# Residual gate prepared beside the spatial stage and kept in DRAM, its memory given to weights and gates, attention's gates two units ahead

## The chip, the cores and the metric

The kernel runs on one core of a Trainium2 chip. Its time is device microseconds of one execution; the time before is the median of three runs, 1124.19 us (1122.96 to 1124.32). The engines are TensorE (PE; its weight loads are shown as PEld), VectorE (DVE), ScalarE (ACT), GpSimd (POOL) and SyncE (SP, which here only issues DMAs; GpSimd issues some as well). Each works off its own queue of instructions in order; they wait for each other on semaphores.

## What is computed

One block of a bidirectional encoder on 1024 tokens of width 1024, all in float32. Cut to what matters:

```
mod = silu(c) @ w_ada + b_ada;  shift, scale, gate = split(mod, 3)
h = rmsnorm(x, norm_g) * (1 + scale) + shift
q, k, v, z_gla, ra_f, ra_b, u, vs, z_gmlp, m_gla, m_gmlp = split(h @ w_in)
log_a = max(log_sigmoid(ra @ alpha_w + alpha_b) / 16, -1.25)       # one per direction
o = gla(q, k, v, log_a_f) + flip(gla(flip(q), flip(k), flip(v), flip(log_a_b), strict))
y_gla = (rmsnorm(o) * gla_norm_g * silu(z_gla)) @ w_br_gla
vs = layernorm(gelu(vs));  sg = per 128 tokens and group: gmlp_ws @ vs + gmlp_bs
y_gmlp = (gelu(u) * sg * silu(z_gmlp)) @ w_br_gmlp
merged = sigmoid(m_gla) * y_gla + sigmoid(m_gmlp) * y_gmlp
out = rmsnorm(x + gate * (merged @ w_out), final_g)
```

gla is gated linear attention in chunks of 64 tokens, 4 heads: b is the running sum of log_a inside a chunk, q * exp(b) and k * exp(-b) give the scores of a chunk, and a state of 128x256 a head is carried on with k * exp(b_last - b) and v.

## The kernel before

Tokens and columns are cut into tiles of 128 and 512. Every product of h or of a branch with a weight is made from high and low halves of both sides (a hi part rounded for TensorE and a lo part for the remainder), hence three matmuls for each: hi x hi, lo x hi, hi x lo. The halves are split by a cast on ScalarE (L175, names ending in h) and a subtraction on VectorE (L176, names ending in l).

The program is written with a tile library. A scheduler simulates it and sets the order of each engine's queue and the slots of each tile; the text is only where it starts from. Tiles live in rings of equal slots: 4 KB a partition for what lasts (h, 30 slots) and for weights (w, 11 slots, `w4`), 2 KB (s, 16 slots, `w2`), 1 KB (q, 12 slots, `w1`). A new tile waits until the last reader of the tile that had its slot is done. The accumulators in PSUM are eight: three `pd`, two `pm`, two `po`, one `pk`.

The stages, by the clock of the profiled execution:

1. Front, 0 to 75 us. Root mean squares of the tokens (`norm_x`, statistics ms at L220), the modulation from w_ada (`ada`), h transposed and split (`make_h`), in three groups of tokens, 0 to 3, 4 and 5, 6 and 7. `spread(g)` (L294) multiplies by a matrix of ones to bring the factors rd of a group's tokens across all partitions. The matmuls of the first half of vs run between.
2. 75 to 180 us: second half of vs (`vs1`), its layer norm, the spatial product (`spatial`, L440 to L450, results sg to DRAM by GpSimd), and v of heads 0 and 1 (`dense_v0`, `dense_v`, L502 to L513; the halves vh, vl lie in the 1 KB ring until SP has stored them).
3. 180 to 600 us: 20 pairs of 128-column blocks of u, z_gmlp, m and z_gla (`pair`). Each is a two by two block product with seven instead of eight multiplications: sums of weights on GpSimd (L574 to L581), sums of h quarters (T1 to T4) made once, and accumulators X (pd), Y (po) and Z (pk). Z is filled by L551 to L553 twice a pair; the last thing read from it is added on VectorE (L607, u), and the next pair's Z starts after that. Between the first pairs stand the residual gate and the small weights of the decay (`low_rank_weights`, kept in ST). The gate multiplies rows of its weights by silu(c) and adds them on VectorE (gacc, L680: eight 512 KB loads wg, one at a time), sums over partitions by a matmul with ones (L689), adds the bias and keeps the row across all partitions in the tile `gate`.
4. 600 to 925 us: attention, 16 units of a head, a direction and half of the tokens. `front_a` makes a unit's gates: decay (L785 on TensorE), three ScalarE activations, a scan on VectorE (L794, L796), then q and k times their exponentials (L810 to L813). `front_b` makes the scores (L822), `front_c` transposes the keys (L832). Four `step`s per unit carry the state (L840 to L842 into pk, L857 and L859 on VectorE) and in the forward direction make the outputs. Between them `dense` takes one piece each of other products from a list of filler jobs: q, k and v of the next heads, and the gMLP branch's output. A unit's gates are made one unit ahead.
5. 925 to 1027 us: the attention branch's output ya (L1156 to L1158), merged with the other branch on VectorE (L1138 to L1141: ta and y2 are read back from DRAM, the merge tile is split into mh and ml). It goes by eight column blocks j and two halves of the tokens.
6. From 1027 us: the output weights (`dense_o`, L211 to L213 with weights th, tl and left side mh, ml). Each of eight 512 KB pieces is loaded (ws), scaled by the gate on GpSimd (L1186) and split. Three tokens begin before the others are ready. x is loaded again (res, L1191, into slots that ya's left side had), added, normalised and stored.

Of the kernel before, what the change touches and what calls it, by code (L numbers as in the profile page):

```python
# [13 lines left out]
ALU = mybir.AluOpType  # L14
# [30 lines left out]
def hybrid_block_kernel(ctx: ExitStack, tc: tile.TileContext, x, wf, wt, wada, wgate, wvr, wst, alpha, abias,  # L45
# [29 lines left out]
    z_d = dram("z_d", [KC, P, T])  # L75
    b12_d = dram("b12_d", [4, P, 1024])
# [35 lines left out]
    ST = cp.tile([P, T], F32R, name="ST")  # L112
    gate = cp.tile([P, D], F32, name="gate")

# [338 lines left out]
    for b in range(2):  # L453
        pw = pm()
        TE.matmul(pw, lhsT=ones, rhs=wsT[:, 4 * b:4 * b + 4, :].rearrange("p g t -> p (g t)"), start=True, stop=True)
        for i in range(4):
            g = 4 * b + i
            V.scalar_tensor_tensor(out=bsb[:, g, :], in0=pw[:, i * P:(i + 1) * P],
                                   scalar=pcol[:, PC_LB + g:PC_LB + g + 1], in1=bsb[:, g, :], op0=ALU.mult,
                                   op1=ALU.add)  # L460
    for t in range(4, 8):
        vs1(t)
    spatial(1)
    for t in range(4):
        vs1(t)
# [41 lines left out]
    def v_steps(acc, pieces, t):  # L507
        for k in range(KC):
            hi, lo = pieces[k]
            TE.matmul(acc, lhsT=H.hi_t(k, t), rhs=hi, start=(k == 0), stop=False)  # L510
            TE.matmul(acc, lhsT=H.hi_t(k, t), rhs=lo, start=False, stop=False)  # L511
            TE.matmul(acc, lhsT=H.lo_t(k, t), rhs=hi, start=False, stop=(k == KC - 1))  # L512
# [152 lines left out]

    def residual_gate():

        gth, gsc = (hp.tile([P, 8], F32, name=n) for n in ("gth", "gsc"))
        V.tensor_scalar(gn, pcol[:, PC_GN:PC_GN + 8], 0.5, None, op0=ALU.mult)
        S.activation(gth, pcol[:, PC_C:PC_C + 8], AF.Tanh, scale=0.5)  # L670
        V.scalar_tensor_tensor(out=gsc, in0=gth, scalar=1.0, in1=pcol[:, PC_C:PC_C + 8], op0=ALU.add, op1=ALU.mult)
        V.tensor_scalar(gsc, gsc, 0.5, None, op0=ALU.mult)
        gacc = ht([P, D], F32, "gacc")
        for k in range(KC):
            wg = ht([P, D], F32, "wg")
            nc.sync.dma_start(wg, wgate[k])
            if k == 0:
                S.activation(gacc, wg, AF.Copy, scale=gsc[:, 0:1])
            else:
                V.scalar_tensor_tensor(out=gacc, in0=wg, scalar=gsc[:, k:k + 1], in1=gacc, op0=ALU.mult, op1=ALU.add)  # L680
        return gacc

    def residual_gate_end(gacc):
        bg = ht([P, D], F32, "bg")
        nc.sync.dma_start(bg, prows[PR_BG].partition_broadcast(P))
        for b in range(2):
            pg = pm()
            sl = slice(b * 512, b * 512 + 512)
            TE.matmul(pg, lhsT=ones, rhs=gacc[:, sl], start=True, stop=True)  # L689
            V.tensor_tensor(out=gate[:, sl], in0=pg, in1=bg[:, sl], op=ALU.add)  # L690

            S.mul(gate[:, sl], gate[:, sl], 0.5)
# [18 lines left out]
    pair_z(2)  # L711
    pair_z(3)
# [317 lines left out]
    def gg_second():  # L1030
# [39 lines left out]
    front_a(0, 0)  # L1070
    dense(3)
    front_b(0, 0)
    dense(1)
    front_c(0, 0)
    for n, (h, u) in enumerate(order):
        q = QUOTA[n]
# [7 lines left out]
        if nxt:  # L1084
            front_a(*nxt)
# [97 lines left out]

    def scale_cols(w, b):
        w3 = w.rearrange("p (k c) -> p k c", k=2)
        G.tensor_tensor(out=w3, in0=w3, in1=gate[:, b * 512:b * 512 + 512].unsqueeze(1).broadcast_to([P, 2, 512]),  # L1186
# [138 lines left out]
```

## Time and profile before

| | |
|---|---|
| time, median of 3 runs | 1124.19 us (1122.96 to 1124.32) |
| profiled execution, own time | 1123.92 us |
| its span | 1121.9 us |
| busy: PE, PEld, DVE, ACT, POOL | 1068.2, 894.4, 641.8, 413.3, 272.7 us |
| moved by DMA | 152.27 MB, 136 GB/s over the span |
| instructions on PE | 5292 matmuls, 5292 weight loads |

The page's busy times are sums over one execution. In rows with an arrow, the left name is the tile that the waiting instruction writes, the right one the instruction that let it go and its line. "Idle before" in square brackets is the time for which the engine had nothing to do ahead of that row. A granted clock of 0.5 means that TensorE ran at half speed.

### The profile page before, as it was taken

Reading aid. Unit: us, or ns where it says so; the run is one execution under the profiler, and the core shown is the slowest. Engines: PE = TensorE matmul, PEld = TensorE weight load, DVE = VectorE, ACT = ScalarE, POOL = GpSimd, SP = SyncE. Lnnn points to the kernel's source line nnn. Section 1 sums busy time; section 2 is a strip of 40 time slices with the busy share of each in tenths; the row PEclk is TensorE's granted clock in tenths of the full one; section 3 lists DMA queues with packets and bytes.
Section 4 is the critical chain, followed back from the end, with each engine's and each line's share of the span. In section 5 each row is a group of like instructions: output and inputs, shape, how many; then the busy total and the mean of one; then the engine's idle time right before and its main releaser. Section 6 shows DMA issues by size and latency. Waiting matters only on the chain.

```text
span 1121.9 us, 14019 instructions
## 1 busy us (share of the span) xinstructions
PE 1068.2 (95%) x5292; PEld 894.4 (80%) x5292; DVE 641.8 (57%) x953; ACT 413.3 (37%) x720; POOL 272.7 (24%) x302
## 2 busy tenths in 40 slices
PE   6889999899999999999999999899989899999997
PEld 4768899678878787877888898798778778888886
DVE  5865568554476555665463466556767664744422
ACT  4453334143332332323233335445536344311222
POOL 2211214443433424343321001001101010012610
PEclk9999999999999999999999999899989899999999
DMA  9541236533233232243336026137525248526112
GB/s 359 186 150 61 85 134 209 192 121 122 75 122 108 100 122 103 92 153 108 118 132 244 1 67 225 39 100 245 191 85 178 86 152 289 189 75 225 38 57 94
DMA packets 55572, 152.27 MB, mean 136 GB/s; under 512 B 7279, under 2 KB 15471, under 8 KB 55506
## 3 DMA queue, kind: packets, MB, share of 16 engines
q1 hardware_dynamic: 40898, 102.42, 26.0%
q0 software_dynamic: 14608, 48.97, 12.2%
q8 instruction: 41, 0.67, 0.2%
q14 instruction: 25, 0.20, 0.1%
HBM read 108.37 MB, written 42.99 MB: 135 GB/s over the span
## 4 chain that ended last, share of the span: by engine, by line
PE 77%; DVE 8%; issue 7%; DMA 3%; ACT 3%; POOL 1%; SPq 0%; POOLq 0%; DVEq 0%; ACTq 0%
PE po L553 4%; PE pd L211 4%; PE pd L212 4%; PE po L551 4%; PE po L552 4%; PE pd L213 4%; PE pd L961 4%; PE pd L962 4%; PE pd L963 4%; PE pk L551 3%; PE pd L553 3%; PE pk L553 3%; PE pd L551 3%; PE pd L552 3%; PE pk L552 3%
## 5 line engine op out<-in xcount | busy, mean ns | idle before, releaser
L511 PE MATMUL pd<-tvl,hh 128*128 128x256 f32 (+1 forms) x256 | 74.6, 292 | 4.0 <-DVE tvl L176 4.0
L510 PE MATMUL pd<-tvh,hh 128*128 128x256 f32 (+1 forms) x256 | 74.7, 292 | 0.8 <-DVE vl L502 0.8
L512 PE MATMUL pd<-tvh,hl 128*128 128x256 f32 (+1 forms) x256 | 74.6, 291 | 0.0
L552 PE MATMUL pd<-hl,ah 128*128 128x512 f32 x160 | 62.3, 390 | 0.0
L553 PE MATMUL pd<-hh,al 128*128 128x512 f32 x160 | 62.2, 389 | 0.0
L551 PE MATMUL pd<-hh,ah 128*128 128x512 f32 x160 | 62.2, 390 | 0.0
L511 PEld LDWEIGHTS pd<-tvl,hh 128*128 128x128 f32 x256 | 49.6, 194 | 4.4 <-DVE tvl L176 4.2
L961 PE MATMUL pd<-ggh,wh 128*128 128x512 f32 x128 | 53.2, 415 | 0.0
L963 PE MATMUL pd<-ggh,wl 128*128 128x512 f32 x128 | 52.1, 408 | 0.0
L962 PE MATMUL pd<-ggl,wh 128*128 128x512 f32 x128 | 51.9, 406 | 0.0
L510 PEld LDWEIGHTS pd<-tvh,hh 128*128 128x128 f32 x256 | 49.6, 194 | 1.3 <-DVE vl L502 1.0
L574 POOL TENSOR_TENSOR wsum<-wb 128x512 f32<-128x512 f32 x20 | 29.5, 1477 | 86.1 <-PE po L552 38.6
L512 PEld LDWEIGHTS pd<-tvh,hl 128*128 128x128 f32 x256 | 49.7, 194 | 0.1
L1158 PE MATMUL pd<-gl,wh 128*128 128x512 f32 x128 | 49.7, 390 | 0.0
L1157 PE MATMUL pd<-gh,wl 128*128 128x512 f32 x128 | 49.7, 389 | 0.0
L1156 PE MATMUL pd<-gh,wh 128*128 128x512 f32 x128 | 49.6, 389 | 0.0
L175 ACT CAST ah<-wa 128x1024 fp32r<-128x1024 f32 x20 | 21.0, 1051 | 73.0 <-PE po L553 52.7
L604 DVE TENSOR_TENSOR p<-po,p 128x512 f32<-128x512 f32 x20 | 13.8, 691 | 58.2 <-PE po L553 58.2
L212 PE MATMUL pd<-tl,mh 128*128 128x512 f32 x120 | 46.8, 391 | 0.0
L221 POOL TENSOR_TENSOR r<-ms,nhalf 128x1 f32<-128x1 f32 (+1 forms) x24 | 20.2, 841 | 109.2 <-DVE ms L220 107.1
L211 PE MATMUL pd<-th,mh 128*128 128x512 f32 x120 | 46.7, 391 | 0.0
L176 DVE TENSOR_TENSOR wl<-ws,wh 128x1024 fp32r<-128x1024 f32 x24 | 29.3, 1221 | 30.2 <-ACT wh L175 16.6
(317 smaller groups left out, 3146.0 us busy)
## 6 DMA issues: line engine op xcount, KB each, us to landing
ws<-in_wf SPq DMA_DIRECT2D x24, 512.0 KB, 4.5
ws<-in_wt SPq DMA_DIRECT2D x22, 512.0 KB, 4.0
wa<-in_wf SPq DMA_DIRECT2D x20, 512.0 KB, 3.6
wb<-in_wf SPq DMA_DIRECT2D x20, 512.0 KB, 4.2
wa<-in_wada SPq DMA_DIRECT2D x16, 512.0 KB, 7.7
xn<-in_x SPq DMA_DIRECT2D x8, 512.0 KB, 8.3
sg_d<-sg POOLq DMA_DIRECT2D x16, 256.0 KB, 2.4
vh_d<-vh SPq DMA_DIRECT2D x32, 128.0 KB, 2.6
```

The costliest lines, as they stand in the source:

```text
L211: TE.matmul(acc, lhsT=xh, rhs=hi[:, k % 2, :], start=(k == 0), stop=False)
L212: TE.matmul(acc, lhsT=xh, rhs=lo[:, k % 2, :], start=False, stop=False)
L510: TE.matmul(acc, lhsT=H.hi_t(k, t), rhs=hi, start=(k == 0), stop=False)
L511: TE.matmul(acc, lhsT=H.hi_t(k, t), rhs=lo, start=False, stop=False)
L512: TE.matmul(acc, lhsT=H.lo_t(k, t), rhs=hi, start=False, stop=(k == KC - 1))
L551: TE.matmul(acc, lhsT=a, rhs=xh(k), start=(first and k == 0), stop=False, skip_group_check=not first)
L552: TE.matmul(acc, lhsT=a, rhs=xl(k), start=False, stop=False, skip_group_check=not first)
L553: TE.matmul(acc, lhsT=b, rhs=xh(k), start=False, stop=(k == 3), skip_group_check=not first)
L961: TE.matmul(acc, lhsT=hi, rhs=x.hi(k, half), start=(k == 0), stop=False)
L962: TE.matmul(acc, lhsT=hi, rhs=x.lo(k, half), start=False, stop=False)
L963: TE.matmul(acc, lhsT=lo, rhs=x.hi(k, half), start=False, stop=(k == KC - 1))
L1157: TE.matmul(acc, lhsT=lo[:, k, :], rhs=GO.hi(k, half), start=False, stop=False)
```

## The change

Seven edits in one:

- The residual gate is worked out between the two halves of the spatial stage, from sixteen loads of 256 KB in 2 KB slots; its matmuls and bias come in the middle of v of head 0, the finished row (2 x 512) is stored to DRAM, and near the end GpSimd loads it again into two 2 KB slots across all partitions.
- The tile `gate` and ST no longer lie in fixed memory: ST takes a weight slot and is made after the third of the last four pairs.
- Rings: weights 11 to 13 slots, 2 KB 16 to 18, 1 KB 12 to 10. v of heads 2 and 3 takes its weights from the weight ring.
- The first pair of u and z comes after the second pair of m.
- Front: the second `spread` comes one step later, the statistics of tokens 6 and 7 come inside the loop.
- Attention: two units' gates are made before the first unit; in the loop those of unit n + 2 come between steps 2 and 3 of unit n.
- The scratch for GpSimd's DMAs is halved.

```diff
-    gate = cp.tile([P, D], F32, name="gate")
-        return hp.tile(shape, dtype, tag="w", bufs=11, name=nm(name))
+        return hp.tile(shape, dtype, tag="w", bufs=13, name=nm(name))
-        return hp.tile(shape, dtype, tag="s", bufs=16, name=nm(name))
+        return hp.tile(shape, dtype, tag="s", bufs=18, name=nm(name))
-        return hp.tile(shape, dtype, tag="q", bufs=12, name=nm(name))
+        return hp.tile(shape, dtype, tag="q", bufs=10, name=nm(name))
...
+        if k == 3:
             spread(1)
-        if k >= 2:
-            make_h(k - 2, 1, abs_[k - 2])
-            steps(k - 2, 1)
-    norm_x(6)
-    norm_x(7)
+        if k == 5:
+            for t in range(6, 8):
+                norm_x(t)
+        for i in {3: (0, 1)}.get(k, (k - 2,) if k > 3 else ()):
+            make_h(i, 1, abs_[i])
+            steps(i, 1)
     spread(2)
...
+    def residual_gate():
...
+        gacc = [w2([P, 512], F32, "gacc") for _ in range(2)]
+        for k in range(KC):
+            for b in range(2):
+                wg = w2([P, 512], F32, "wg")
+                nc.sync.dma_start(wg, wgate[k, :, b * 512:b * 512 + 512])
+                if k == 0:
+                    S.activation(gacc[b], wg, AF.Copy, scale=gsc[:, 0:1])
+                else:
+                    V.scalar_tensor_tensor(out=gacc[b], in0=wg, scalar=gsc[:, k:k + 1], in1=gacc[b], op0=ALU.mult,
+                                           op1=ALU.add)
+        return gacc
+
+    def residual_gate_end(gacc, ins):
+        with tc.issue_after(ins.ins):
+            pg = [pm() for _ in range(2)]
+            for b in range(2):
+                TE.matmul(pg[b], lhsT=ones, rhs=gacc[b], start=True, stop=True)
+        for b in range(2):
+            bg = w2([P, 512], F32, "bg")
+            nc.sync.dma_start(bg, prows[PR_BG, b * 512:b * 512 + 512].partition_broadcast(P))
+            V.tensor_tensor(out=bg, in0=pg[b], in1=bg, op=ALU.add)
+            S.mul(bg, bg, 0.5)
+            nc.sync.dma_start(gate_d[b:b + 1, :], bg[0:1, :])
...
     spatial(1)
+    gacc = residual_gate()
...
+            if t == TOKENS[4]:
+                residual_gate_end(gacc, i)
...
+        ST = w4([P, T], F32R, "ST")
...
     pair_m(FB_MB, tb_d, 0)
-    gacc = residual_gate()
     pair_m(FB_MB, tb_d, 1)
+    pair_uz(0)
     pair_m(FB_MB, tb_d, 2)
     pair_m(FB_MB, tb_d, 3)
-    residual_gate_end(gacc)
-    low_rank_weights()
-    pair_uz(0)
     pair_uz(1)
...
     pair_z(2)
+    ST = low_rank_weights()
     pair_z(3)
...
-            (lambda: v_weights(2, ht), run_v(2)),
+            (lambda: v_weights(2, w4), run_v(2)),
-            (lambda: v_weights(3, ht), run_v(3)),
+            (lambda: v_weights(3, w4), run_v(3)),
...
-    front_a(0, 0)
-    dense(3)
-    front_b(0, 0)
+    front_a(*order[0])
+    dense(2)
+    front_a(*order[1])
     dense(1)
-    front_c(0, 0)
+    front_b(*order[0])
+    dense(1)
+    front_c(*order[0])
...
-        if nxt:
-            front_a(*nxt)
...
         step(h, u, 2)
+        if n + 2 < len(order):
+            front_a(*order[n + 2])
         dense(1)
...
+    gate = [w2([P, 512], F32, "gate") for _ in range(2)]
+    for b in range(2):
+        G.dma_start(gate[b], gate_d[b].partition_broadcast(P))
...
-    nc = _bacc.Bacc("TRN2", target_bir_lowering=False, num_devices=1, dynamic_dma_scratch_size=4096)
+    nc = _bacc.Bacc("TRN2", target_bir_lowering=False, num_devices=1, dynamic_dma_scratch_size=2048)
```

The edits shift lines by up to 35 in the changed text, and the scheduler orders anew. Three places in its order follow; each row is a line, an operation, the tile it writes and those it reads. Numbers behind names only tell tiles of one name apart.

TensorE between two pairs, before: pk_2019 is one pair's Z, pk_2152 the next one's, pd_2226 the next one's X.

```order
1097 L552 MATMUL pk_2019<-hl_108,fh_1956 128x512
1098 L553 MATMUL pk_2019<-hh_107,fl_1957 128x512
1099 L551 MATMUL pd_2226<-hh_93,ah_2209 128x512
1100 L552 MATMUL pd_2226<-hl_94,ah_2209 128x512
1101 L551 MATMUL pk_2152<-t0h_1468,sh_2080 128x512
1102 L552 MATMUL pk_2152<-t0l_1469,sh_2080 128x512
```

And now, from the same pair's last Z product (1099) to the next one's first (1112):

```order
1099 L589 MATMUL pk_2057<-hh_106,fl_1995 128x512
1100 L589 MATMUL pd_2258<-hh_92,al_2242 128x512
1101 L587 MATMUL pd_2258<-hh_92,ah_2241 128x512
1102 L588 MATMUL pd_2258<-hl_93,ah_2241 128x512
1103 L589 MATMUL pd_2258<-hh_92,al_2242 128x512
1104 L587 MATMUL pd_2258<-hh_96,ah_2241 128x512
...
1110 L587 MATMUL po_2273<-t1h_1544,sh_2245 128x512
1111 L588 MATMUL po_2273<-t1l_1545,sh_2245 128x512
1112 L587 MATMUL pk_2190<-t0h_1537,sh_2120 128x512
```

Two matmuls between became twelve: ten more of X and two of Y were drawn ahead. Over all 19 boundaries the number was 2 nine times, 4 once, 8 four times and 22 or 24 five times; now it is 12 or more at each.

VectorE in attention, before, at the second split of v's weights for head 3 (tvl_5618, for matmuls that come right after the state product pk_5702): the rows L801 to L813 are the gates of the next unit, L859 state steps of the running one.

```order
575 L801 COPY c_978_5576<-b_5574 128x8
576 L859 SCALAR_TENSOR_TENSOR s_5706<-s_5687,dec_5403,pk_5702 128x256
577 L807 TENSOR_TENSOR b_5574<-b_5574,c_978_5576 128x4x64
578 L806 TENSOR_TENSOR dec_5580<-e_979_5578 128x4
579 L811 TENSOR_TENSOR qh_5583<-qh_5583,qk_4688 128x512
580 L176 TENSOR_TENSOR tvl_5618<-ws_5615,tvh_5617 128x1024
581 L813 TENSOR_TENSOR b_5574<-b_5574,qk_4769 128x512
```

And now (tvl_5647 is the same split, L867 the state step, L809 to L821 the gates of the same unit):

```order
573 L815 TENSOR_TENSOR b_5570<-b_5570,c_983_5572 128x4x64
574 L867 SCALAR_TENSOR_TENSOR s_5552<-s_5515,dec_5163,pk_5548 128x256
575 L174 TENSOR_TENSOR tvl_5647<-ws_5644,tvh_5646 128x1024
576 L814 TENSOR_TENSOR dec_5576<-e_984_5574 128x4
577 L819 TENSOR_TENSOR qh_5579<-qh_5579,qk_4717 128x512
578 L844 TENSOR_TENSOR kel_5610<-pm_5604,keh_5609 128x512
579 L821 TENSOR_TENSOR b_5570<-b_5570,qk_4798 128x512
...
588 L867 SCALAR_TENSOR_TENSOR s_5687<-s_5654,dec_5374,pk_5683 128x256
```

The gates and the split stand ahead of the running unit's state steps, which come from row 588 on; the state step at row 574 belongs to the unit before it.

The end, SP and ScalarE. Before, SP (in_wt are output weights, res is x, ta the merge's factor of the last column block, second half):

```order
245 L169 DMA ws_8307<-in_wt 128x1024
246 L169 DMA ws_8314<-in_wt 128x1024
247 L169 DMA ws_8321<-in_wt 128x1024
248 L169 DMA ws_8328<-in_wt 128x1024
249 L1191 DMA res_8404<-in_x 128x1024
...
256 L1191 DMA res_8598<-in_x 128x1024
257 L1136 DMA ta_8298<-ta_d 128x512
258 L1137 DMA y_1507_8297<-y_d 128x512
```

And now:

```order
254 L167 DMA ws_8340<-in_wt 128x1024
255 L1145 DMA ta_8292<-ta_d 128x512
256 L1146 DMA y_1513_8291<-y_d 128x512
257 L1204 DMA res_8437<-in_x 128x1024
...
264 L1204 DMA res_8631<-in_x 128x1024
265 L1145 DMA ta_8327<-ta_d 128x512
266 L1146 DMA y_1518_8326<-y_d 128x512
267 L167 DMA ws_8347<-in_wt 128x1024
268 L167 DMA ws_8354<-in_wt 128x1024
269 L167 DMA ws_8361<-in_wt 128x1024
```

ScalarE before (th is a piece of the output weights, mh a merge tile):

```order
604 L175 CAST th_8324<-ws_8321 128x1024
605 L1140 CAST mh_8186<-ta_8189 128x512
606 L1140 CAST mh_8186<-ta_8222 128x512
607 L175 CAST th_8331<-ws_8328 128x1024
608 L1140 CAST mh_8260<-ta_8263 128x512
609 L1140 CAST mh_8295<-ta_8298 128x512
```

And now:

```order
604 L1149 CAST mh_8215<-ta_8218 128x512
605 L1149 CAST mh_8215<-ta_8251 128x512
606 L1149 CAST mh_8289<-ta_8292 128x512
607 L1149 CAST mh_8324<-ta_8327 128x512
608 L173 CAST th_8343<-ws_8340 128x1024
609 L173 CAST th_8350<-ws_8347 128x1024
```

Of the first four pieces of the output weights, three moved behind x and the last ta, and their casts behind the last merge tile. VectorE's four subtractions tl moved likewise. On TensorE three products with th_8343 stand right behind the last product of ya, then the first with tl_8344.

More of the change, by code (lines that the diff above doesn't have):

```diff
@@ L75, in hybrid_block_kernel @@
     z_d = dram("z_d", [KC, P, T])
+    gate_d = dram("gate_d", [2, 512])
     b12_d = dram("b12_d", [4, P, 1024])
@@ L110, in hybrid_block_kernel @@
     pcol = cp.tile([P, NPC], F32, name="pcol")
-    ST = cp.tile([P, T], F32R, name="ST")
-    gate = cp.tile([P, D], F32, name="gate")
     gn = cp.tile([P, 8], F32, name="gn")
@@ L460, in hybrid_block_kernel @@
                                    op1=ALU.add)
+    def residual_gate():
+        gth, gsc = (hp.tile([P, 8], F32, name=n) for n in ("gth", "gsc"))
+        V.tensor_scalar(gn, pcol[:, PC_GN:PC_GN + 8], 0.5, None, op0=ALU.mult)
+        S.activation(gth, pcol[:, PC_C:PC_C + 8], AF.Tanh, scale=0.5)
+        V.scalar_tensor_tensor(out=gsc, in0=gth, scalar=1.0, in1=pcol[:, PC_C:PC_C + 8], op0=ALU.add, op1=ALU.mult)
+        V.tensor_scalar(gsc, gsc, 0.5, None, op0=ALU.mult)
+        gacc = [w2([P, 512], F32, "gacc") for _ in range(2)]
[20 more added lines that the diff above has]
+            nc.sync.dma_start(gate_d[b:b + 1, :], bg[0:1, :])
     for t in range(4, 8):
@@ L511, in v_steps @@
             TE.matmul(acc, lhsT=H.hi_t(k, t), rhs=lo, start=False, stop=False)
-            TE.matmul(acc, lhsT=H.lo_t(k, t), rhs=hi, start=False, stop=(k == KC - 1))
+            i = TE.matmul(acc, lhsT=H.lo_t(k, t), rhs=hi, start=False, stop=(k == KC - 1))
+        return i
     TOKENS = (4, 5, 6, 7, 0, 1, 2, 3)
@@ L518, in dense_v0 @@
             acc = pd()[:, 0:NV0]
-            v_steps(acc, v0_w, t)
+            i = v_steps(acc, v0_w, t)
+            if t == TOKENS[4]:
+                residual_gate_end(gacc, i)
             S.copy(ra[:, t, :], acc[:, HV:NV0])
@@ L664, in low_rank_weights @@
                                in1=sa[96:128, :], op0=ALU.mult, op1=ALU.add)
[L666 to L692, printed above, removed]
+        return ST
     pair_m(FB_MB, tb_d, 0)
-    gacc = residual_gate()
     pair_m(FB_MB, tb_d, 1)
+    pair_uz(0)
     pair_m(FB_MB, tb_d, 2)
     pair_m(FB_MB, tb_d, 3)
-    residual_gate_end(gacc)
-    low_rank_weights()
-    pair_uz(0)
     pair_uz(1)
@@ L1069, in hybrid_block_kernel @@
     dense(4)
-    front_a(0, 0)
-    dense(3)
-    front_b(0, 0)
+    front_a(*order[0])
+    dense(2)
+    front_a(*order[1])
     dense(1)
-    front_c(0, 0)
+    front_b(*order[0])
+    dense(1)
+    front_c(*order[0])
     for n, (h, u) in enumerate(order):
-        q = QUOTA[n]
         nxt = order[n + 1] if n + 1 < len(order) else None
@@ L1094, in hybrid_block_kernel @@
         step(h, u, 1)
-        dense(q - 3)
+        dense(QUOTA[n] - 3)
         if nxt:
@@ L1182, in hybrid_block_kernel @@
     ms = [None] * NT
+    gate = [w2([P, 512], F32, "gate") for _ in range(2)]
+    for b in range(2):
+        G.dma_start(gate[b], gate_d[b].partition_broadcast(P))
     def scale_cols(w, b):
         w3 = w.rearrange("p (k c) -> p k c", k=2)
-        G.tensor_tensor(out=w3, in0=w3, in1=gate[:, b * 512:b * 512 + 512].unsqueeze(1).broadcast_to([P, 2, 512]),
+        G.tensor_tensor(out=w3, in0=w3, in1=gate[b].unsqueeze(1).broadcast_to([P, 2, 512]),
                         op=ALU.mult)
```

## The prediction

> **What bounds the kernel now.** I read the busy totals first, then who made TensorE wait, then the same time by stages.
>
> ```profile
> PE 1068.2 (95%) x5292; PEld 894.4 (80%) x5292; DVE 641.8 (57%) x953; ACT 413.3 (37%) x720; POOL 272.7 (24%) x302
> ```
>
> TensorE is the bound: 95% busy. The change leaves its products as they are, so all that can move is its idle time, 1121.9 - 1068.2 = 53.7 us, and the time in which it runs at half clock. The view of waits, for TensorE alone (total us, times, longest):
>
> ```profile
> PE pm L822 <- DVE b L813: 6.1, 2, 4.0
> PE pk L551 <- DVE u L607: 6.1, 13, 1.0
> PE pd L511 <- DVE tvl L176: 4.0, 1, 4.0
> PE pm L689 <- DVE gacc L680: 3.9, 1, 3.9
> PE pm L294 <- DVE ms L220: 3.3, 1, 3.3
> PE pk L840 <- DVE s L859: 3.0, 6, 0.8
> PE pm L294 <- DVE rd L260: 2.0, 1, 2.0
> ```
>
> Nearly all of it ends on VectorE, at places where TensorE's queue has too little work between a request and its answer. By stages (length, busy us and count of TensorE, weight loads, VectorE, ScalarE, GpSimd, then granted clock, DMA share, GB/s):
>
> ```profile
> core 0: us, PE busy (x) PEld busy (x) DVE busy (x) ACT busy (x) POOL busy (x), PEclk, DMA share, GB/s
> 0.00:75.00 75.00, 57.80 (x252) 43.78 (x253) 50.03 (x110) 34.84 (x59) 18.82 (x22) 1.00 0.58 219
> 75.00:180.00 105.00, 105.00 (x644) 94.52 (x643) 68.61 (x113) 38.10 (x59) 19.53 (x29) 1.00 0.37 130
> 180.00:240.00 60.00, 53.39 (x278) 44.23 (x277) 36.51 (x38) 19.08 (x28) 28.20 (x25) 0.97 0.52 167
> 240.00:600.00 360.00, 353.92 (x1540) 287.44 (x1539) 204.42 (x236) 120.97 (x168) 133.29 (x146) 1.00 0.33 115
> 600.00:700.00 100.00, 99.31 (x581) 87.40 (x581) 50.09 (x91) 43.30 (x87) 6.49 (x11) 1.00 0.38 136
> 700.00:730.00 30.00, 24.54 (x146) 22.15 (x145) 17.15 (x29) 13.25 (x30) 2.73 (x4) 0.89 0.10 36
> 730.00:800.00 70.00, 69.18 (x428) 61.86 (x427) 45.67 (x81) 40.41 (x86) 7.77 (x13) 1.00 0.56 185
> 800.00:830.00 30.00, 24.11 (x111) 19.88 (x110) 17.83 (x30) 9.09 (x19) 3.06 (x6) 0.83 0.30 106
> 865.00:885.00 20.00, 17.54 (x75) 13.94 (x74) 11.81 (x21) 8.06 (x17) 3.26 (x5) 0.83 0.44 144
> 885.00:925.00 40.00, 37.97 (x200) 31.14 (x199) 27.62 (x50) 14.88 (x37) 4.32 (x7) 1.00 0.34 114
> 925.00:1027.00 102.00, 101.96 (x458) 84.37 (x458) 53.58 (x70) 31.09 (x48) 12.35 (x8) 1.00 0.53 185
> ```
>
> Idle (length less busy): front 17.2, the gate's stretch 180 to 240 6.6, the pairs 6.1, attention 0.7 + 5.5 + 0.8 + 5.9 + 2.5 + 2.0 = 17.4, then none up to 1027. The clock falls below 1 just where the long waits are. Cut finer, the stretches behind two of the 4.0 us waits, and the spacing of 256-wide matmuls before and in the first of them:
>
> ```profile
> 721.40:727.50 6.10, 6.10 (x29) 6.10 (x30) 0.93 (x2) 0.94 (x3) 0.00 (x0) 0.51 0.14 47
> 816.80:823.00 6.20, 6.16 (x19) 5.22 (x20) 3.84 (x7) 0.62 (x1) 0.55 (x1) 0.50 0.12 45
> ```
>
> ```profile
> 711.91 0.28 PE L512 MATMUL pd<-tvh,hl 128*128 128x256 f32 x1
> 712.03 0.28 PE L510 MATMUL pd<-tvh,hh 128*128 128x256 f32 x1
> ...
> 722.17 0.41 PE L511 MATMUL pd<-tvl,hh 128*128 128x256 f32 x1
> 722.38 0.41 PE L512 MATMUL pd<-tvh,hl 128*128 128x256 f32 x1
> ```
>
> Full busy, but at 0.21 us a matmul in place of 0.12: of each 0.21 us 0.09 is lost, 43%. So a wait of 4.0 us costs 4.0 + 0.43 x 6.1 = 6.6 us. [...]
>
> **The change, part by part.** The sum is made against the profiled execution's own 1123.92 us (span 1121.9 and 2.0 around it); the median of the runs, 1124.19, is 0.3 above it. A measurement of this kernel can tell about 0.2%, 2.2 us, from no change.
>
> *Front.* The second spread now comes one step later, and the statistics of tokens 6 and 7 two steps earlier. The waits at stake are the 3.3 (ms) and 2.0 us (rd) of L294. The first should go: VectorE gets that work with more than a step of matmuls ahead of it; the second may only shift. Bounds 0 and -5.3; I take -3.0, little short of the one wait that loses its cause. Work saved here does reach the end, since 75 to 180 is 105.00 busy of 105.
>
> *Residual gate.* Its matmul waits 3.9 us at L689, and products held up by the same VectorE queue bring the stretch to 6.6 us idle; clock 0.97 of 60 us is 1.8 us short, that is 3.6 us at half clock, worth 0.43 x 3.6 = 1.5. All that goes: 8.1 us. The cause is a chain of loads, one at a time (view of waits, VectorE):
>
> ```profile
> DVE gacc L680 <- DMA wg<-in_wgate: 17.7, 7, 5.2
> ```
>
> The work returns inside 120 to 180: 14 sums of 128x512 at about 0.69 us (a row of that form stands below) are 9.7 us more on VectorE, whose 68.6 of 105 become 78; and 16 loads, 4 MB, enter SP's queue ahead of nearly all stores of v, at 130 GB/s moved so far. What waits behind them: the stores free ten small slots, enough for five tokens of v, then VectorE stops at the next low half, and TensorE after its three accumulators. That cover is eight tokens of work; if it fails I put the loss at one landing as slow as below (9.9 us) less what is covered. Bounds 0 and +8; I take +1.7, because the loads' slots come free before v begins. Sum -6.4. Writing the row to DRAM and reading it back adds four small transfers with nothing due for hundreds of us: 0.
>
> *Pairs.* The 6.1 us of L551 behind u (L607) are 13 waits of up to 1.0 us: one accumulator, two matmuls of cover (the order shows 2, 4 or 8 at the boundaries that wait). Now at least 12 stand there; the spacing of 512-wide matmuls is 0.23 us (1027.15 to 1027.38, quoted below), so cover grows by 10 x 0.23 = 2.3 us, more than the longest wait. Bounds 0 and -6.1; I take -5.5. The two extra 4 KB slots are what lets the next weights be split that early.
>
> *Attention.* Gates two units ahead: in VectorE's order the weight split tvl that cost 4.0 us now stands ahead of the state steps that it used to follow, and the scores' operands (L813) come a unit earlier. At stake 17.4 us idle and half clock: (0.11 x 30 + 0.17 x 30 + 0.17 x 20) / 0.5 = 23.6 us, of which TensorE idled through 0 to 10 (the three long waits are 10.1); 0.43 x 23.6 = 10.1 down to 0.43 x 13.6 = 5.8, say 7.9. What stays: the last units, where no filler is left (2.0 in 885 to 925), and new short waits, since a unit's last state steps now queue behind the gates of two units on: 3.0 (as much as L859 costs today). One of the three half-clock stretches I leave in. So -(17.4 - 5.0) - 7.9 x 2/3 = -17.7; bounds -25.3 and 0.
>
> *The end: a new wait.* In SP's order three of the four first-half pieces of the output weights moved behind eight loads of x (4 MB); in ScalarE's order all four casts (th), in VectorE's all four remainders (tl) moved behind the last tile of the merge. Before, these casts were interleaved and TensorE went straight over. The rows there:
>
> ```profile
> 1022.75 1.05 ACT L175 CAST th<-ws 128x1024 fp32r<-128x1024 f32 x1 [3.01 <-POOL ws L1186]
> ```
>
> ```profile
> 1027.15 0.39 PE L1158 MATMUL pd<-gl,wh 128*128 128x512 f32 x1
> 1027.38 0.39 PE L211 MATMUL pd<-th,mh 128*128 128x512 f32 x1
> 1027.41 1.22 DVE L176 TENSOR_TENSOR tl<-ws,th 128x1024 fp32r<-128x1024 f32 x1 [2.37 <-PE pd L1157]
> ...
> 1033.10 0.69 DVE L1138 SCALAR_TENSOR_TENSOR ta<-ta,pd 128x512 f32<-128x512 f32 x1 [4.46 <-DMA ta<-ta_d]
> 1033.82 0.69 DVE L1139 TENSOR_TENSOR ta<-ta,y 128x512 f32<-128x512 f32 x1
> 1034.55 0.62 ACT L1140 CAST mh<-ta 128x512 fp32r<-128x512 f32 x1 [10.23 <-DVE ta L1139]
> ...
> 1035.05 2.40 POOL L1186 TENSOR_TENSOR ws<-ws,gate 128x1024 f32<-128x1024 f32 x1 [12.34 <-DMA ws<-in_wt]
> ```
>
> ```profile
> res<-in_x SPq DMA_DIRECT2D x8, 512.0 KB, 7.9
> ...
> ta<-ta_d SPq DMA_DIRECT2D x1, 256.0 KB, 9.9
> ```
>
> The last tile ta is loaded behind the x loads and lands 9.9 us after its issue, so VectorE reaches it at 1033.10 and the cast mh ends at 1035.17. Today that hurts nobody: the first cast stood ahead of it, and three tokens of matmuls ran meanwhile. Now th comes next: 1035.2 + 1.05 = 1036.2, against 1027.38: 8.8 us of idle. Three matmuls need th alone (0.7 us), the fourth tl, 1.22 after th: +0.6. Then half clock, as behind the 4.0 us waits: 0.43 x 6.1 = 2.6. Together +12.0. The next pieces keep up: each feeds 18 matmuls, 4.1 us, and costs GpSimd 2.40. Bounds: +8.8 without the rest, and +16 if the three pieces issued right behind (1.5 MB) delay ta as the 4 MB ahead of it do: 9.9 x 1.5 / 4 = 3.7.
>
> *Smaller edits.* Halved scratch for GpSimd's DMAs, slots moved between sizes: 0. [...]
>
> Sum: 1123.9 - 3.0 - 6.4 - 5.5 - 17.7 + 12.0 = 1103.3.
>
> **The rivals.**
>
> *The end hardly stalls*, because ta lands like the other fifteen. Its loads by landing:
>
> ```profile
> DMA to landing us min/median/max: 2.6/3.8/9.9
> ```
>
> At 3.8 the 8.8 us shrink to 2.7, with 0.6 for tl and no half clock: 1103.3 - 12.0 + 3.3 = 1095; with no stall at all 1091. For it: the first piece itself is loaded ahead of x. Against: the maximum is this very load, behind the same eight.
>
> *Attention's waits only move.* Two units' gates must be held at once, while the ring of small slots shrank from 12 to 10; if they come free too late, VectorE does the gates no earlier than today. Then attention yields perhaps 3 us: 1103.3 + 14.7 = 1118. Against: the waits named above each have their cause moved in the order.
>
> *Slower: the gates get in front of the state.* Place: VectorE between a unit's third and fourth state step. The gates' work there, from first to last row today:
>
> ```profile
> 810.85 0.69 DVE L790 SCALAR_TENSOR_TENSOR e<-pm,e 128x512 f32<-128x512 f32 x1
> ...
> 814.56 0.16 DVE L806 TENSOR_TENSOR dec<-e 128x4 f32<-128x4 f32 x1
> ```
>
> 3.9 us, 0.9 of it state steps: 2.9 us in front of the state that TensorE's next product needs. Exposed in 14 units, that is 41 us in place of the 25.3 lost now: 1103.3 + 17.7 + 41 - 25.3 = 1137. Slower than 1126.1 it is from (25.3 + 1126.1 - 1121.0) / 14 = 2.2 us per unit, when hardly any filler stands between; one filler piece of eight matmuls covers 1.8 of the 2.9, which is why I think it unlikely.
>
> *It does not do what it says:* the gate's loads cost in v what they saved (+6.4) and the front only shifts (+3): 1113, still faster.
>
> **How the numbers follow.** Forecast 0.55 with its own range 1095 to 1113 (bounds of the parts, not all at one end); little or no stall at the end 0.13; attention only moved 0.17; slower by the state 0.08; the gate and front idle 0.07. Range 1088 to 1120, leaving out the slower case, half of what is beyond 1118, and the lowest corner. Faster 0.87; within 0.2% 0.04, from the upper edge of the attention rival; slower 0.09.
>
> **What would show it.** Right: no wait on gacc; the waits behind u gone or under 1 us in all; clock 1.00 from 600 to 900; a gap of 9 to 13 us between the last merge product (L1165 to L1167 now) and the first product of the output weights, with a half-clock stretch behind it. Wrong: waits on the state (s) growing past 10 us, an idle stretch in the v products, or no gap at the end.

## The result

The changed kernel takes 1096.08 us (median of 4 runs, 1094.35 to 1098.20) against 1123.58 us of the kernel before beside it: 0.976 of the time, 95% interval 0.973 to 0.979. It is faster by 2.4%. The forecast was 1103.3 with a range of 1088 to 1120; the gain was forecast as 20.6 us and is 27.5.

The busy totals of the changed kernel:

```profile
PE 1057.6 (97%) x5292; PEld 892.7 (82%) x5292; DVE 641.1 (59%) x960; ACT 412.1 (38%) x721; POOL 276.1 (25%) x304
```

TensorE does the same 5292 matmuls; in a span of 1095.3 us it idles 37.7 us, where it idled 53.7. Of the 26.6 us that the span lost, 16.0 are idle time and 10.6 are busy time. Little of the 10.6 is half clock: the mean granted clock is 0.987 over the span before and 0.988 over this one, short of full clock by 14.6 us and 13.1 us, a difference of 1.5. The rest is mostly starts of matmuls that come late while the row of the matmul ahead still counts as busy; for the pairs this is worked out further below. The view of waits of the changed kernel, TensorE alone (total us, times, longest):

```profile
PE pd L209 <- ACT th L173: 7.8, 1, 7.8
PE pd L241 <- DMA crow<-in_prows: 4.2, 1, 4.2
PE pd L210 <- DVE tl L174: 3.5, 1, 3.5
PE pm L830 <- DVE b L821: 2.6, 1, 2.6
PE pm L306 <- DVE rd L258: 2.0, 2, 1.1
...
PE pd L969 <- ACT wh L173: 1.8, 1, 1.8
...
PE pk L587 <- DVE u L643: 1.1, 1, 1.1
```

The waits on gacc, on tvl and on ms are gone, that on u (13 times before) happens once. What leads the list now is new: th and tl at the start of the output weights. The second row is the first matmul of all, which waits for its input in both kernels. The same by stages (length, busy us and count of TensorE, weight loads, VectorE, ScalarE, GpSimd, then granted clock, DMA share, GB/s):

```profile
0.00:75.00 75.00, 62.48 (x260) 48.37 (x261) 50.26 (x109) 34.69 (x58) 19.49 (x21) 0.95 0.58 223
75.00:180.00 105.00, 105.00 (x648) 94.38 (x647) 78.45 (x129) 41.35 (x63) 22.25 (x32) 1.00 0.49 171
180.00:240.00 60.00, 60.00 (x314) 51.33 (x313) 25.78 (x34) 20.06 (x30) 20.77 (x21) 1.00 0.34 115
240.00:600.00 360.00, 358.86 (x1579) 295.01 (x1578) 203.97 (x241) 125.64 (x172) 140.52 (x155) 1.00 0.37 128
600.00:700.00 100.00, 100.00 (x638) 90.54 (x637) 64.42 (x116) 52.64 (x115) 7.56 (x12) 1.00 0.31 105
700.00:800.00 100.00, 99.42 (x591) 87.30 (x590) 71.36 (x124) 49.98 (x109) 10.28 (x17) 1.00 0.47 158
800.00:925.00 125.00, 119.22 (x600) 100.13 (x599) 77.60 (x123) 53.90 (x114) 13.83 (x21) 0.99 0.54 184
925.00:1020.00 95.00, 83.65 (x353) 68.14 (x352) 43.80 (x47) 15.60 (x25) 20.89 (x11) 0.93 0.35 124
```

180 to 240 is full, the pairs idle 1.1 us in place of 6.1, and attention from 700 on has a clock of 1.00 and 0.99 where the same two stretches had 0.97 and 0.93 before. The front idles 12.5 us in place of 17.2, but at a clock of 0.95 in place of 1.00. The stretch that clearly got worse is the last: 11.4 us idle and a clock of 0.93.

To set the terms of the prediction against this I worked out a loss for each stage: the distance from one matmul's start to the next, less what it is at full speed (0.227 us for 512 columns, 0.120 for 256, 0.112 for 128: the medians between neighbours of one width in the trace of before), summed over the stage. It holds idle time, half clock and every other delay of TensorE.

| stage | loss before, us | loss now, us | change | term of the prediction |
|---|---|---|---|---|
| front, 0 to 75 | 25.6 | 23.2 | -2.3 | -3.0 |
| vs and v, 75 to 182 | 1.4 | 2.2 | +0.8 | with the gate |
| gate's stretch, 182 to 240 | 9.8 | 0.2 | -9.6 | -6.4, both rows |
| pairs, 240 to 600 | 11.3 | 3.0 | -8.2 | -5.5 |
| attention (to 925; now to 900) | 43.1 | 22.0 | -21.1 | -17.7 |
| ya and output weights | 1.8 | 15.5 | +13.7 | +12.0 |
| sum | | | -26.7 | -20.6 |

The span fell by 26.6. Every sign is right; all but the front's term were too small. The table sets one execution against one other. In three more executions with the order of before (one of the same kernel, two with only the scratch halved, all below) the same sum gives 25.8 to 28.1 us for the front and 39.9 to 41.7 for attention, so a row's change can be off by 2 or 3 us.

### The profile page after: what moved, and what is told of

It reads as the page before. It is cut to its first block, busy times and chain, and to the rows that moved or that the text cites. A ratio compares the mean times of both kernels' runs of the same rounds, so it can differ in the third digit from the quotient of the medians.

```text
span 1095.3 us, 14011 instructions
## 1 busy us (share of the span) xinstructions
PE 1057.6 (97%) x5292; PEld 892.7 (82%) x5292; DVE 641.1 (59%) x960; ACT 412.1 (38%) x721; POOL 276.1 (25%) x304
## 3 DMA queue, kind: packets, MB, share of 16 engines
q0 software_dynamic: 14768, 49.50, 12.5%
## 4 chain that ended last, share of the span: by engine, by line
PE 81%; DVE 5%; issue 5%; DMA 4%; ACT 2%; POOL 1%; SPq 0%; POOLq 0%; ACTq 0%; DVEq 0%
PE pd L210 5%; PE pd L211 5%; PE po L589 4%; PE po L587 4%; PE po L588 4%; PE pd L209 4%; PE pd L969 4%; PE pd L970 4%; PE pd L971 4%; PE pk L587 3%; PE pk L589 3%; PE pk L588 3%; PE pd L587 3%; PE pd L588 3%; PE pd L589 3%
## 5 line engine op out<-in xcount | busy, mean ns | idle before, releaser
L174 DVE TENSOR_TENSOR al<-wa,ah 128x1024 fp32r<-128x1024 f32 x20 | 31.4, 1571 | 32.7 <-PE po L588 30.8
L610 POOL TENSOR_TENSOR wsum<-wb 128x512 f32<-128x512 f32 x20 | 25.8, 1288 | 94.2 <-DMA wb<-in_wf 69.7
L211 PE MATMUL pd<-th,ml 128*128 128x512 f32 x120 | 48.0, 400 | 0.0
```

What stands on the lines that cost most here:

```text
L211: return TE.matmul(acc, lhsT=xl, rhs=hi[:, k % 2, :], start=False, stop=(k == KC - 1))
```

## The experiments

The theory: five separate parts, each with the price of its own wait, and at the end a stall that the new order brought in. Each kernel below undoes or adds one of them. Where nothing else is said, the comparison is with the changed kernel's 1096.1 us. The kernel before took 1123.6 us beside that, and 1121.3 or 1123.0 beside the kernels compared with it here, so a difference of 2 us may be nothing.

### The output weights ahead of x

```diff
+            a = S.copy(flat(hi), w)              # tm_weights, keeping its instructions
+            wlog.append((i, a, d))
...
-        nc.sync.dma_start(res[t], x[t * P:(t + 1) * P, :])
+        with tc.issue_after(wlog[-1][0].ins):
+            nc.sync.dma_start(res[t], x[t * P:(t + 1) * P, :])
```

The pieces, and the gate's row that scales them, are also asked for ahead of the last merge tile in the text. The scheduler then spread loads, casts and remainders over the merge, as before the change.

> The changed kernel with one more edit at its end: x is loaded again only after the four first-half pieces of the output weights have been issued, so that pieces, casts and remainders stand between the merge tiles as they did before the change. Theory (the 7.8 and 3.5 us waits at the start of the output weights, with the half clock behind them, are the order's own price): the stretch from the last merge product on loses its 15.2 us against full speed but for some 1.5, time 1096.1 - 13.7 = 1082 to 1083. Rival (x then comes too late and VectorE waits for it at the first additions, so that the wait only moves): 1088 or more, with TensorE waiting for an accumulator.

1081.3 us (1078.3 to 1085.1), 0.963 of the kernel before (0.960 to 0.966): 14.8 us better than the change alone. By stages, the stretch in which the stall stood:

```profile
960.00:1010.00 50.00, 50.00 (x222) 41.31 (x221) 26.27 (x29) 11.01 (x19) 16.69 (x10) 1.00 0.39 147
```

50.00 busy of 50 at full clock; the loss from 960 to 1020 is 0.1 us in place of 15.3. The wait did not move to x. So the stall was the order's price, and this version beats both kernels. Whether the edge on x or the earlier place in the text did it, this run does not tell apart.

### The last merge factor ahead of x

```diff
-        nc.sync.dma_start(y2, y2_d[j, :, sl])
+        ta_last[0] = nc.sync.dma_start(y2, y2_d[j, :, sl])
...
-        nc.sync.dma_start(res[t], x[t * P:(t + 1) * P, :])
+        with tc.issue_after(ta_last[0].ins):
+            nc.sync.dma_start(res[t], x[t * P:(t + 1) * P, :])
```

> The changed kernel with one edit: the last merge factor ta and its partner y2 are loaded ahead of the eight loads of x instead of behind them; pieces and casts stay where they are. Theory (two causes share the loss: the casts stand behind the last merge tile, and that tile's load lands 9.3 us late behind 4 MB of x): the first wait shrinks from 7.8 to about 3 us (0.7 + 0.7 + 0.6 for the merge tile, 1.0 for the cast), but the second piece still lands behind x and makes TensorE wait some 3 us once more; 4 to 5 us gained, 1091 to 1092. Rival A (the order of the casts alone costs it all): no change, 1096. Rival B (the late landing is all of it): 1084.

1088.8 us (1086.6 to 1089.3): 7.3 us better, between the theory and rival B. This is the changed kernel's trace at the place, TensorE, ScalarE, VectorE and GpSimd (start, duration, and in brackets the idle time before and its end):

```profile
985.50 0.39 PE L1167 MATMUL pd<-gl,wh 128*128 128x512 f32 x1
...
993.72 1.65 PE L209 MATMUL pd<-th,mh 128*128 128x512 f32 x3 [7.83 <-ACT th L173]
...
998.89 0.80 PE L210 MATMUL pd<-tl,mh 128*128 128x512 f32 x1 [3.52 <-DVE tl L174]
```

```profile
990.66 0.69 DVE L1147 SCALAR_TENSOR_TENSOR ta<-ta,pd 128x512 f32<-128x512 f32 x1 [7.37 <-DMA ta<-ta_d]
...
992.75 2.80 DVE L1150 TENSOR_TENSOR ml<-ta,mh 128x512 fp32r<-128x512 f32 x1 [0.68 <-ACT mh L1149]
995.48 11.12 DVE L174 TENSOR_TENSOR tl<-ws,th 128x1024 fp32r<-128x1024 f32 x4
```

```profile
992.10 0.62 ACT L1149 CAST mh<-ta 128x512 fp32r<-128x512 f32 x1 [9.54 <-DVE ta L1148]
992.63 1.04 ACT L173 CAST th<-ws 128x1024 fp32r<-128x1024 f32 x1
```

```profile
958.84 2.41 POOL L1199 TENSOR_TENSOR ws<-ws,gate 128x1024 f32<-128x1024 f32 x1 [1.93 <-PE pd L1167]
992.64 8.41 POOL L1199 TENSOR_TENSOR ws<-ws,gate 128x1024 f32<-128x1024 f32 x3 [31.39 <-DMA ws<-in_wt]
```

The first piece was scaled at 958.84; for 31 us it only stood behind the merge tile in ScalarE's queue. And with ta first:

```profile
989.11 1.23 DVE L174 TENSOR_TENSOR tl<-ws,th 128x1024 fp32r<-128x1024 f32 x1 [0.25 <-ACT th L173]
...
989.13 0.97 PE L209 MATMUL pd<-th,mh 128*128 128x512 f32 x3 [3.10 <-ACT th L173]
...
990.39 0.65 PE L210 MATMUL pd<-tl,mh 128*128 128x512 f32 x1 [0.29 <-DVE tl L174]
991.69 11.43 POOL L1201 TENSOR_TENSOR ws<-ws,gate 128x1024 f32<-128x1024 f32 x4 [30.36 <-DMA ws<-in_wt]
...
997.56 0.50 PE L210 MATMUL pd<-tl,mh 128*128 128x512 f32 x1 [1.19 <-DVE tl L174]
```

The first wait is 3.10 as expected. The second is 0.29 in place of 3.52, since ml and the first tl now come before GpSimd begins to scale, and the tl takes 1.23 us in place of some 2.8; that I had not counted. The third piece of the theory, TensorE waiting again for the second weight piece, is the 1.19. The loss at the end is 7.1 us where it was 15.3 and, in the experiment above, 0.1. So about half of the stall comes from ta landing behind x. The other half stays with ta first; the casts behind the merge tile and the second piece behind x share it, and no run parts them.

### Attention's gates one unit ahead, in both directions

In the changed kernel, undone:

```diff
-        if n + 2 < len(order):
-            front_a(*order[n + 2])
...
+        if nxt:
+            front_a(*nxt)
         last = order[n - 1] if n and SEQ[order[n - 1][1]][0] else None
```

> The changed kernel with attention's gates made one unit ahead as before, all else as changed. Theory (the attention gain is the two units ahead and nothing else): the loss against full speed between 600 us and the end of attention goes back from 22 to about 43 us, time 1096.1 + 21 = 1117. Rival (the gain came from the larger rings, weights for v in their own ring included): at most +5, 1101.

1112.4 us (1110.7 to 1113.0): 16.3 us worse. Its waits and two of its stages:

```profile
PE pm L830 <- DVE b L821: 4.6, 2, 4.0
...
PE pk L848 <- DVE s L867: 3.1, 5, 1.0
```

```profile
700.00:800.00 100.00, 91.40 (x536) 79.84 (x535) 68.05 (x119) 48.54 (x102) 10.88 (x18) 0.97 0.44 156
800.00:925.00 125.00, 118.43 (x607) 99.36 (x605) 81.36 (x133) 57.45 (x126) 15.42 (x25) 0.99 0.50 173
```

The scores' wait of 4.0 us and the waits on the state are back. Of the 21 us I expected 16.3 came: the loss of attention went to 36.9, not to 43.1.

> The kernel before with attention's gates made two units ahead and nothing else changed (16 slots of 2 KB, 12 of 1 KB). Theory: -21, 1123.6 - 21 = 1102 to 1103, since the place in VectorE's order is what counts. Rival (without the two more 2 KB slots the gates of two units cannot be held, and they are made as late as before): -5 at most, 1118.

1104.8 us (1103.7 to 1108.0), against 1121.3 of the kernel before beside it, 0.984 (0.983 to 0.986): 16.5 us better, without any of the larger rings. Stages of it:

```profile
700.00:800.00 100.00, 98.03 (x600) 87.87 (x599) 68.11 (x118) 54.50 (x119) 12.62 (x20) 0.98 0.46 158
800.00:925.00 125.00, 120.69 (x632) 101.39 (x631) 83.55 (x141) 56.02 (x126) 16.55 (x26) 1.00 0.49 169
```

The loss of attention there is 22.3, the same as with the whole change. So in both directions the place of the gates is worth 16 us, and the two 2 KB slots are not needed for it: the rival falls. That the loss of attention says 21 and the time 16.5 has its cause elsewhere: in the profiled execution of this kernel, whose span is 18.5 us shorter than that of before, the front lost 1.9 us more and the gate's stretch 1.3, neither of which the edit touches; and the profiled execution of before took 1123.9 us, 2.6 more than the median here, with the largest attention loss of the four of its order.

The 6 us between 36.9 and 43.1 have the size of one wait, that of TensorE for tvl (4.0 us, 6.6 with its half clock by the prediction's sum). It is in the list of neither kernel, the one with gates one unit ahead and all else changed, or this one. So gates two units ahead are enough to remove it, but some other part of the change is too: with one unit ahead v's last weight split begins at 683.9 us, in the kernel before at 720.1. Which part, perhaps the weights of v in the weight ring, no run shows.

### The front's old order

```diff
-        if k == 3:
             spread(1)
-        if k == 5:
-            for t in range(6, 8):
-                norm_x(t)
...
+    norm_x(6)
+    norm_x(7)
     spread(2)
```

> The changed kernel with the front's order as before (second spread one step earlier, statistics of tokens 6 and 7 after the loop). Theory: the wait of 3.3 us for the statistics comes back, and 2.3 us net, 1098.4. Rival (the front's gain was a shift that later work swallows): no change, within 1 us.

1100.0 us (1096.7 to 1100.9): 3.9 us worse, where 2.3 were expected. Against the kernel before the ratio is 0.979 (0.976 to 0.982), that of the whole change 0.976 (0.973 to 0.979), so the times alone hardly part the two. The waits of it that answer:

```profile
PE pm L292 <- DVE ms L218: 3.3, 1, 3.3
PE pm L306 <- DVE rd L258: 2.3, 3, 1.1
PE pm L292 <- DVE rd L258: 1.9, 1, 1.9
```

Both waits of L294 before (3.3 and 2.0) are back with their sizes, and the loss up to 75 us is 27.1 in place of 23.2, with another 1.1 in a gap that ends just behind 75. Over all profiled executions the same sum is 25.6 to 28.1 us in the six with the old order of the front and 22.2 to 23.7 in the six with the new one, some 4 us apart on the mean. So the gain of the front is real, and as TensorE has next to no idle time from 75 to 180 in either order (105.00 and 104.49 busy of 105), nothing there swallows it.

### The residual gate at its old place

```diff
     spatial(1)
-    gacc = residual_gate()
...
     pair_m(FB_MB, tb_d, 0)
+    gacc = residual_gate()
...
     pair_m(FB_MB, tb_d, 3)
+    residual_gate_end(gacc)
```

> The changed kernel with the residual gate made where it was before, among the first pairs (loads after the first pair, matmuls after the fourth), still in 256 KB loads and 2 KB slots and by way of DRAM. Theory (the gain was the place): 6 to 9.6 us come back, 1102 to 1106, with TensorE waiting for gacc or for the u tiles of the first pairs. Rival (the smaller loads, two of them in flight, and the freed 4 KB slots were the gain): no change, 1096.

1101.8 us (1100.7 to 1105.6): 5.7 us worse, just under the 6 to 9.6 of the theory and far from the rival's nothing. By stages and waits:

```profile
180.00:240.00 60.00, 56.48 (x282) 47.11 (x281) 28.16 (x40) 16.49 (x25) 18.87 (x17) 0.97 0.51 172
```

```profile
PE po L583 <- DVE u L625: 2.4, 1, 2.4
```

TensorE waits for a u tile behind VectorE's sums, as before, but no longer for gacc itself. The loss of the stretch is 6.6 where the kernel before had 9.8. So of the 9.6 us some 6.4 are the place. The other 3.2 stayed won; whether by the smaller loads, of which several are under way at a time (in the changed kernel all 16 are issued from 133.3 to 148.9 us, and the median load lands 5.3 us after its issue), or by the ten matmuls more between the pairs, no run tells apart.

### Eleven weight slots

```diff
-        return hp.tile(shape, dtype, tag="w", bufs=13, name=nm(name))
+        return hp.tile(shape, dtype, tag="w", bufs=11, name=nm(name))
```

> The changed kernel with 11 instead of 13 slots for weights. Its order has 2 matmuls again between two Z accumulations at eleven of nineteen boundaries. Theory (the pairs gained by the two slots, which let the next pair's X be drawn ahead): the pairs' loss goes from 3.0 back to about 11 us, time 1096.1 + 8 = 1104. Rival (the pairs gained by the moved gate and by the first pair of u and z coming earlier): +2 at most, 1098.

1104.0 us (1102.1 to 1105.1): 7.9 us worse, as the theory had it. Its waits, and the pairs' stage:

```profile
PE pk L587 <- DVE u L643: 7.6, 14, 1.2
```

```profile
240.00:600.00 360.00, 352.92 (x1538) 286.69 (x1537) 208.31 (x240) 123.99 (x172) 134.97 (x154) 1.00 0.34 120
```

14 waits on u where there was one, and 7.1 us of idle in the stage; the loss of the pairs is 12.3 in place of 3.0. The stall at the end stays (th 7.4, tl 3.5 us): it does not come from the weight ring. What made the scheduler move the casts is left open; none of these kernels (front, gate's place, attention, ring) has its end in the old order. The gates two units ahead alone do not bring the stall: the kernel before with only that edit loses 0.3 us from 925 us on. The gate's row read back near the end is a part of the change that no run undid.

### The halved scratch

```diff
-    nc = _bacc.Bacc("TRN2", target_bir_lowering=False, num_devices=1, dynamic_dma_scratch_size=4096)
+    nc = _bacc.Bacc("TRN2", target_bir_lowering=False, num_devices=1, dynamic_dma_scratch_size=2048)
```

Made alone in the kernel before, twice, with the kernel before timed against itself beside the second:

> The kernel before with the halved scratch for GpSimd's DMAs alone. Theory: nothing, 1123.6 within 0.2%. Rival (each GpSimd issue waits for the one ahead): longer issues on GpSimd than 0.55 us, and several us slower.

> The kernel before, unchanged, timed against itself. It tells how far the comparison strays where nothing differs. Theory (the 0.28% found for the halved scratch is noise between programs that do the same): a ratio within 0.3% of 1, its interval perhaps clear of 1. Rival (the halved scratch really costs 0.28%): a ratio within 0.1% of 1 here, and 1.002 to 1.004 again for the scratch.

> The kernel before with the halved scratch alone, again. Theory (noise): a ratio between 0.998 and 1.002. Rival (a real cost): 1.002 to 1.004 again.

The ratios: 1.0028 (1.0013 to 1.0043) at first, 1.0014 (0.9999 to 1.0030) the second time; the kernel against itself 0.9991 (0.9977 to 1.0005). An issue on GpSimd takes as long as before (groups of the kernel with the halved scratch: line, transfer, count, busy us and mean ns):

```profile
L627 POOL DMA_DIRECT2D sgl<-sg_d x16 | 8.9, 556 | 0.2 <-issue 0.2
```

556 ns, where it was 557. The cost lies between nothing and 0.4%; the two runs cannot tell more, and the trace shows no mechanism for it.

## Why the prediction was right, point by point

**The bound.** Right that TensorE's products stay as they are and that its idle time moves. Not complete: I let only idle time and half clock move. Of the span's 26.6 us idle time gave 16.0 and clock some 1.5; the 9 us left are mostly late starts inside busy rows, for which I had no term (see the pairs).

**Front, -3.0.** Measured -2.3 in the trace; undoing it alone cost 3.9 us. The place is right. Both waits of L294 on VectorE went, not one, and idle time fell by 4.7 us; but the clock of 0.95 over 75 us is 3.75 short, some 7.5 us at half clock, 0.43 of it 3 us lost. The half clock stood in no term, so that the pair of executions comes out near -3.0 is partly luck. The new order does not always bring it: the kernel with the output weights ahead of x has the same edit of the front, and a clock of 1.00 there.

**Residual gate, -6.4 with 1.7 for the loads ahead of v.** Measured -9.6 at its old place and +0.8 at the new one. The fear for the stores of v did not come true: 105.00 busy of 105. VectorE's sums there took 753 ns each, not 0.69, and filled it to 78.45 of 105, as worked out.

**Pairs, -5.5.** Measured -8.2, above the upper bound of 6.1. The step that failed is the price of a wait. Rows of the kernel before at one of the thirteen:

```profile
326.77 0.39 PE L552 MATMUL pd<-hl,ah 128*128 128x512 f32 x1
328.15 0.50 PE L551 MATMUL pk<-t0h,sh 128*128 128x512 f32 x1 [0.99 <-DVE u L607]
328.49 0.40 PE L552 MATMUL pk<-t0l,sh 128*128 128x512 f32 x1
```

The row says 0.99 us idle. But the start before it is 1.38 us back where 0.23 would do, 1.15 lost, and the next start comes 0.34 later, 0.11 more: 1.26 us. A matmul's row is 0.39 us long while the next one starts 0.23 after it where nothing waits (326.54 and 326.77 us), so idle time counted from the end of the last row leaves out 0.16 us of the wait, and the restart cost 0.11 here. Over 12 waits fewer, (8.2 - 4.9 of idle) / 12 = 0.27 us each. I took the idle column for the whole price, here and for the short waits of the other terms.

**Attention, -17.7.** Measured -21.1 in the trace, against the slowest of four executions of the old order; 16 us are shown to be the two units ahead. For the wait on tvl I gave the gates' place in VectorE's order as the cause; it also stays away without that, so another part of the change would have removed it too. Idle time fell from 17.4 to 0.0 + 0.6 + 5.8 = 6.4, so 11.0 where I put 12.4. The half clock went almost wholly (0.01 of 125 us short in the last stage) where I had left a third of it, and the waits that went may have taken along what they cost beyond their idle time, as in the pairs (0.27 us each there). What stays is where I named it, in the last units: 2.6 us on the scores of the last one is the longest. The new short waits on the state, 3.0 in the sum, did not come (0.2 us).

**The end, +12.0.** Measured +13.7, and 14.8 when taken away. Place and cause were right, and the 8.8 us of idle nearly so (7.83 by the row; 993.72 - 985.50 - 0.23 = 8.0 by the starts). Mis-sized was the wait for tl, 3.52 in place of 0.6: VectorE's ml took 2.80 us instead of 0.69, and the four tl took 11.12 / 4 = 2.78 each instead of 1.22, while GpSimd scaled three weight pieces from 992.64 on (with ta first, and GpSimd idle, the first tl took 1.23). The row that would have told stood in the timeline of before, next to the scaling that began at 1035.05; I quoted the scaling and not its neighbour:

```profile
1035.20 2.79 DVE L1141 TENSOR_TENSOR ml<-ta,mh 128x512 fp32r<-128x512 f32 x1 [0.69 <-ACT mh L1140]
```
The half clock, 2.6 in the sum, ran through that second wait:

```profile
985.70:994.70 9.00, 1.17 (x3) 0.83 (x3) 3.33 (x3) 1.56 (x2) 2.06 (x1) 0.78 0.89 354
994.70:1004.20 9.50, 5.98 (x15) 4.20 (x14) 9.50 (x5) 3.13 (x3) 8.05 (x4) 0.50 0.27 85
1004.20:1010.00 5.80, 5.80 (x26) 4.79 (x25) 2.40 (x1) 0.00 (x0) 4.39 (x2) 0.98 0.68 226
```

9.5 us at 0.50, of which TensorE worked 6.0. As the second wait stands inside this stretch, it does not tell how long the half clock lasts behind one wait alone.

**Smaller edits, 0.** An estimate of mine; the runs put the halved scratch between nothing and 0.4%, with issues of 556 ns where they were 557.

**The rivals.** The end did stall. The "no half clock" behind 2.7 us, with which the first rival was priced, was an estimate too: behind the 2.6 us wait on the scores 3.4 us of half clock followed, behind the 3.3 us for ms in the kernel before none. Attention's waits did not move; the gates in front of the state cost nothing that shows, for the waits on the state are all but gone (0.2 us, where they were 3.0).

**The signs named.** No wait on gacc: so it is. The waits behind u under 1 us in all: one of 1.1. Clock 1.00 from 600 to 900: but for 3.4 us of half clock behind that 2.6 us wait on the scores. A gap of 9 to 13 us before the output weights: 8.2 by the starts, and the wait for tl stands behind it. So three of the four signs missed narrowly. Of the signs of being wrong none appeared.

**What the parts add up to.** Undone alone, attention's place costs 16.3 us, the ring 7.9, the gate's place 5.7 and the front 3.9; the end, mended, gives 14.8 back. That is 19.0 of the 27.5 us gained. The 8.5 left, of the size of the 3.2 and 6 us left over above, may hang on parts that no run undid by themselves (the smaller gate loads, v's weights in the weight ring, the first pair's place, ST) or on parts that cover for each other.

## What to carry to other kernels

Price a wait by the distance between the starts of two matmuls, less what it is at full speed, and not by the idle time in the row: here that was 0.27 us more for each short wait of the pairs. Of the waits of 2.6 to 4.0 us some cost 1.2 to 2.7 more here for the clock (2.8 to 6.2 us of work at half clock, 0.43 of it lost), and one of 3.3 nothing. When an edit changes memory or order, read the order at the places where transfers crowd, as the load of x does here: one tile that landed 9.3 us after its issue (the median of its sixteen is 3.6) and a cast queued behind it took back a third of what the change had won. A single ordering edge on x gave half of that back, and asking for the weights early as well as ahead of x gave all of it. If two engines' long instructions can meet (GpSimd's scaling and VectorE's splits), take the duration of the one from a row where the other runs: tl took 1.23 us with GpSimd idle and 2.78 beside the scaling.

## What the runs showed of the hardware

VectorE's instructions took up to four times as long beside GpSimd's scaling of 128x1024: ml 0.69 and 2.80 us, tl 1.23 (with ta first, GpSimd idle) and 2.78. GpSimd's own took 2.41 us beside one addition of VectorE and 2.80 (8.41 / 3) beside ml and the splits. The addition in the changed kernel:

```profile
959.45 2.35 DVE L1148 TENSOR_TENSOR ta<-ta,y 128x512 f32<-128x512 f32 x1
```

Elsewhere it takes 0.69; here it began inside the scaling (958.84 to 961.25) and ended 0.55 us behind it. The addition took 1.7 us more than elsewhere and ml 2.1, each most of one scaling; no run shows what in the hardware makes them longer.

The half clock behind two waits of 4.0 us in the kernel before (721.4, 816.8) lasted 6 us of work (6.10 us at a clock of 0.51, 6.16 at 0.50). But behind its wait of 3.9 us for gacc it lasted 2.9 us:

```profile
222.30:226.20 3.90, 0.01 (x1) 0.00 (x0) 1.38 (x2) 0.24 (x1) 1.86 (x3) 0.93 0.54 200
226.20:229.10 2.90, 2.84 (x5) 1.32 (x5) 1.20 (x2) 1.62 (x3) 0.54 (x1) 0.51 0.57 201
```

With ta first the wait of 3.10 us has this behind it:

```profile
985.00:1004.00 19.00, 14.41 (x54) 10.82 (x53) 12.04 (x7) 4.71 (x5) 12.31 (x5) 0.91 0.64 247
```

0.09 of 19 us short is 3.4 us at half clock. The wait of 2.6 us on the scores in the changed kernel also has 3.4 us of half clock behind it, and the one of 3.3 us for ms in the front of the kernel before has none (1.00 over 0 to 75). So in these traces a wait's length alone does not tell whether half clock follows, or for how long.
